# Router products on rows without their norm factor: a change to a two-layer trunk on one Trainium2 core

## The chip, the cores and the metric

The kernel runs on one core of one Trainium2 chip. The metric is the device time of one execution in microseconds (us). The engines are called as in the profile: PE is TensorE, DVE is VectorE, ACT is ScalarE, POOL is GpSimd, SP is SyncE. SP issues nearly all loads; ACT and POOL issue some transfers of their own.

## The reference

The model is a diffusion trunk of two layers over 512 latent and 256 context tokens of width 1024. Each layer mixes the tokens in four ways (attention, neighbourhood attention, a state-space scan, retention), projects the mix with `w_out`, adds it to the stream, and then sends every token to 2 of 32 experts. What the change touches is between the projection and the experts:

```python
xl = xl + gt1 * (jnp.concatenate([a_l, n_l, s_l, r_l], axis=-1) @ w_out[layer])
...
fl = rmsnorm(xl, g_ffn[layer]) * (1.0 + sc2) + sh2
...
def moe_ffn(h, w_group, b_group, w_expert, b_expert, w1, w3, w2):
    g_logits = jnp.matmul(h, w_group, preferred_element_type=F32) + b_group
    g_prob = jax.nn.softmax(g_logits, axis=-1)
    g_idx = jnp.argmax(g_logits, axis=-1)
    e_logits = (jnp.matmul(h, w_expert, preferred_element_type=F32) + b_expert).reshape(T, MOE_GROUPS, MOE_EXPERTS_PER_GROUP)
    e_logits = jnp.take_along_axis(e_logits, g_idx[:, None, None], axis=1)[:, 0]
    top_p, top_i = lax.top_k(jax.nn.softmax(e_logits, axis=-1), MOE_TOP_K)
...
        return (jax.nn.silu(xb @ w1[e]) * (xb @ w3[e])) @ w2[e]
```

`rmsnorm` divides a row by the root of its mean square, so `fl` is, row by row, `x * r * A2 + sh2` with one factor r per row and two vectors A2 and sh2 per layer and stream (latent or context). The router's 36 logits (4 groups, 4 x 8 experts) are `fl @ w_r + b_r`. All of it is in float32.

## The kernel before, in words

The stream lies in SBUF as row tiles of 128 tokens: six in layer 0 (four latent, two context), four in layer 1, where the context is no longer needed. A row tile is `xr`, 128 x 1024.

After the mixers, `w_out` (L1206 to L1245) is called for all row tiles with half 0 (columns 0 to 511 of the output), then for all with half 1. A call makes 24 products `wo_ps` of 128x512 (L202 to L204: each float32 operand is split into a high and a low part, and three products of the parts are added), multiplies by the gate `gt1` into the one buffer `wot` (L1223) and adds to `xr` (L1224). Half 1 goes on with the norm and the router. ACT squares the whole row into the new tile `h` and sums (L1229); DVE scales and adds epsilon (`rs_a`, L224), POOL raises to -1/2 (`rs_b`, L226); DVE makes h = x * r * A2 (L1231) and adds sh2 (L1232), 128x1024 each; ACT issues the write of the row tile `h` to the DRAM tensor `hd` (L1233), from which layer 0's experts gather their rows. In layer 1 the tile is also split into `hx`. PE transposes `h` in eight blocks (`h_t`, L1240), ACT copies them to `h2T` (L1242), eight products with the router weights `w_r` give `r_ps` (L1244), and DVE adds `b_r` into the logits `lgt` (L1245). The tile `h` has two buffers, taken in turn. A third writer of the same buffer waits until the readers of the first, the row write among them, are done.

The rows gt1, A2 and sh2 of each stream are loaded by SP from the DRAM tensor `md`, spread over all partitions (`mrow`, issued at the first call). Behind them on SP stand the expert weights: 1 MB tiles `ew` (L1406), six per expert. Some are loaded ahead into buffers that come free while `w_out` runs. Seven of them start when half 0 is done.

When all logits are there, `route` (L1266) runs on DVE: three times the first maximum of 4 or 8 values (`argmax`, L1247 to L1264, six operations: maximum, equal to it, two operations that turn the mask into an index or a large number, minimum, one-hot), softmax factors, counts and slots. A check for overflow reads a value to the engines' registers and branches (L1808, L1810), and the experts begin.

The order of the instructions on each engine isn't written by hand: a scheduler takes the program and arranges it, so the router work of a row tile is placed among the output products of the next.

## Time and profile before

| | |
|---|---|
| median of 3 runs | 2256.13 us (2254.74 to 2261.66) |
| profiled execution | 2260.11 us, span 2258.3 us |
| mean granted TensorE clock | 0.938 |
| busy: PE, DVE, ACT, POOL | 1955.8, 933.0, 499.6, 370.0 us |
| moved by the DMA engines | 578.55 MB, mean 256 GB/s |
| last output product of `w_out`, layer 0 and 1 | starts at 607.37 and 1720.13 us |
| first product of an expert in layer 0 | starts at 649.00 us |

A timeline row gives the start in us from the span's start, the duration, engine, line, operation, and in brackets the engine's idle time before it and what ended that. A windows row gives the busy time of each engine in a stretch. Granted clock is TensorE's, as a share of its full speed. A queue row (q1 SP's, q10 ACT's) gives the packets in a stretch, the MB, and their share of the time of the 16 DMA engines.

### The profile page before, as it was taken

The page shows a single profiled execution, that of the slowest core. Times are in us where ns is not written, and L with a number is a line of the kernel's source. Part 1 is how long each engine was busy: PE and PEld are TensorE (multiplying, and loading weights), DVE is VectorE, ACT ScalarE, POOL GpSimd, SP SyncE. Part 2 cuts the span into 40 slices and gives each one's busy share as a digit, 9 for nine tenths or more (in the row PEclk, how much of TensorE's full clock was granted, in tenths as well). Part 3 has the DMA queues.
Part 4 walks back from the last instruction along what each step waited for, and adds up shares of the span by engine and source line. Part 5 has one row for each costly group of instructions (what it writes and reads, how often), then busy time and mean ns, then how long its engine had stood idle before and what let it go on. Part 6 is the DMA issues. An engine that isn't in the chain of part 4 may idle for free. (4 is left out here: it accounts for less than half of the span.)

```text
span 2258.3 us, 32874 instructions
## 1 busy us (share of the span) xinstructions
PE 1955.8 (87%) x12609; PEld 1161.1 (51%) x12609; DVE 933.0 (41%) x2175; ACT 499.6 (22%) x1095; POOL 370.0 (16%) x396
## 2 busy tenths in 40 slices
PE   5897988899869879989887887988896898998996
PEld 2787865457733323333332687855475454444443
DVE  3758156463425411111111529056544353453444
ACT  3342232251202200000001521332432111111111
POOL 2532252120100000000001322253302000000000
PEclk9898999999979999999998988989997899999998
DMA  7351355562568999999998441355617599999996
GB/s 271 107 150 44 83 175 195 194 202 71 191 248 305 376 391 375 385 375 362 373 373 342 154 105 49 83 166 192 202 59 269 216 395 419 419 420 418 419 420 255
DMA packets 160477, 578.55 MB, mean 256 GB/s; under 512 B 30032, under 2 KB 71504, under 8 KB 111152
## 3 DMA queue, kind: packets, MB, share of 16 engines
q1 hardware_dynamic: 123344, 530.69, 61.8%
q10 hardware_dynamic: 31296, 31.36, 4.5%
q0 software_dynamic: 5664, 14.23, 2.2%
q8 instruction: 104, 1.70, 0.3%
q14 instruction: 69, 0.57, 0.1%
HBM read 536.33 MB, written 43.42 MB: 257 GB/s over the span
## 5 line engine op out<-in xcount | busy, mean ns | idle before, releaser
L1671 PE MATMUL e_pa<-ew,hT 128*64 128x512 f32 x1664 | 424.4, 605 | 39.0 <-DMA ew<-in_moe_w 32.5
L1671 PEld LDWEIGHTS e_pa<-ew,hT 128*64 128x64 f32 x1664 | 126.2, 139 | 299.0 <-issue 245.1
L1695 PE MATMUL e_py<-ew,aT 128*64 128x512 f32 x832 | 207.1, 632 | 10.6 <-DVE aT L1687 7.8
L226 POOL TENSOR_TENSOR rs_b<-rs_a,mhalf 128x1 f32<-128x1 f32 (+1 forms) x58 | 38.2, 658 | 834.5 <-DVE rs_a L224 829.5
L202 PE MATMUL nat_ps<-w_hi,hTh 128*128 128x272 f32 (+3 forms) x480 | 149.4, 311 | 9.0 <-ACT nat L190 5.5
L1676 ACT ACTIVATE sA<-e_pa 64x512 f32<-64x512 f32 x52 | 30.8, 592 | 564.0 <-PE e_pa L1671 549.9
L1677 DVE TENSOR_TENSOR sA<-sA,e_pa 64x512 f32<-64x512 f32 x52 | 35.9, 690 | 277.2 <-ACT sA L1676 276.7
L204 PE MATMUL nat_ps<-w_hi,hTl 128*128 128x272 f32 (+3 forms) x480 | 147.1, 306 | 0.0
L203 PE MATMUL nat_ps<-w_lo,hTh 128*128 128x272 f32 (+3 forms) x480 | 146.8, 306 | 0.0
L197 POOL TENSOR_TENSOR w_lo<-w_raw,w_hi 128x1024 fp32r<-128x1024 f32 (+2 forms) x36 | 89.9, 2509 | 234.2 <-ACT w_hi L196 109.7
L1695 PEld LDWEIGHTS e_py<-ew,aT 128*64 128x64 f32 x832 | 59.0, 143 | 113.9 <-issue 95.2
L1557 POOL DMA_INDIRECT hg<-hd,stok x32 | 31.3, 980 | 446.2 <-PE hg_t L1569 411.9
L202 PEld LDWEIGHTS nat_ps<-w_hi,hTh 128*128 128x128 f32 x480 | 98.9, 206 | 10.7 <-ACT nat L190 6.4
L296 PE MATMUL mod_ps<-wmod,cT 128*32 128x256 f32 x768 | 80.1, 444 | 27.2 <-DMA wmod<-in_w_mod 27.2
L192 DVE COPY hT<-hg_t 128x256 f32<-128x256 f32 (+2 forms) x45 | 24.0, 534 | 192.0 <-PE e_pa L1671 160.6
L203 PEld LDWEIGHTS nat_ps<-w_lo,hTh 128*128 128x128 f32 x480 | 98.7, 206 | 0.4 <-issue 0.4
L204 PEld LDWEIGHTS nat_ps<-w_hi,hTl 128*128 128x128 f32 x480 | 98.4, 205 | 0.2 <-issue 0.2
L203 PE MATMUL tr_ps<-hTl,w_hi 128*128 128x256 f32 (+1 forms) x256 | 88.1, 344 | 11.0 <-POOL hTl L486 10.6
L202 PE MATMUL tr_ps<-hTh,w_hi 128*128 128x256 f32 (+1 forms) x256 | 88.1, 344 | 5.4 <-DVE gT L583 3.3
L204 PE MATMUL tr_ps<-hTh,w_lo 128*128 128x256 f32 (+1 forms) x256 | 85.5, 334 | 0.0
L1017 PE MATMUL pT_ps<-const,sm_p 128*128 128x128 f32 x352 | 57.6, 292 | 18.4 <-DVE sm_p L1007 12.1
L1642 DVE TENSOR_TENSOR xr<-xr,po_ps 128x512 f32<-128x512 f32 x104 | 67.1, 684 | 7.7 <-PE po_ps L1640 7.1
(471 smaller groups left out, 3530.6 us busy)
## 6 DMA issues: line engine op xcount, KB each, us to landing
ew<-in_moe_w SPq DMA_DIRECT2D x384, 1024.0 KB
wmod<-in_w_mod SPq DMA_DIRECT2D x96, 512.0 KB
yd<-zero SPq DMA_DIRECT2D x20, 512.0 KB
w_raw<-in_w_in SPq DMA_DIRECT2D x16, 544.0 KB
w_raw<-in_w_in SPq DMA_DIRECT2D x16, 512.0 KB
w_raw<-in_w_out SPq DMA_DIRECT2D x32, 256.0 KB
yd<-yA ACTq DMA_DIRECT2D x64, 128.0 KB
hd<-h ACTq DMA_DIRECT2D x10, 512.0 KB
```

The lines of the kernel that those rows point to most:

```text
L197: (eng or self.nc.vector).tensor_tensor(out=lo, in0=src, in1=_f(hi), op=ALU.subtract)
L202: mm(out, lhsT=lh, rhs=rh, start=start, stop=False)
L203: mm(out, lhsT=lh, rhs=rl, start=False, stop=False)
L204: mm(out, lhsT=ll, rhs=rh, start=False, stop=stop)
L226: nc.gpsimd.tensor_tensor(out=r, in0=t, in1=self.mhalf[:, :n], op=ALU.pow)
L296: nc.tensor.matmul(ps[32 * j:32 * j + 32, 256 * q:256 * q + 256], lhsT=self.cT[:, k], rhs=w[:, j], start=(k == 0), stop=(k == KD - 1))
L1017: nc.tensor.transpose(pt[:, b], p[:, (a + b) * P:(a + b + 1) * P], self.ident)
L1557: self.nc.gpsimd.indirect_dma_start(out=hg, out_offset=None, in_=self.hd[0:n], in_offset=bass.IndirectOffsetOnAxis(ap=idx, axis=0), bounds ...
L1642: nc.vector.tensor_tensor(out=x, in0=x, in1=ps, op=ALU.add)
L1671: mm(pa[64 * j:64 * j + 64], lhsT=hT[k][:, 0:64], rhs=(w1, w3)[j][k], start=(k == 0), stop=(k == KD - 1))
L1677: nc.vector.tensor_tensor(out=sA, in0=sA, in1=pa[64:128], op=ALU.mult)
L1695: mm(py[64 * j:64 * j + 64, 0:512], lhsT=aT[:, k * 64:(k + 1) * 64], rhs=w2[k][:, h * 512:(h + 1) * 512], start=(k == 0), stop=(k == 3))
```

## The change

1. The transposes and router products take g = x * A2, without r and sh2. The logits are then r_ps * r + rb, where rb = sh2 @ w_r + b_r is one row of 36 per stream, on all partitions. g is made in two column halves. `h` is finished in the same tile, g * r + sh2, behind that.
2. The mean square is taken by column halves: ACT squares 128x512 after each half's addition, into the `wot` buffer; `ms2` keeps the first half's sum, DVE adds (`n_a`) and POOL raises (`n_b`).
3. rb is made in `router_bias`, at the first call: ACT issues a read of sh2 from `md` by columns, 128 x 8 single elements per stream (`sh2c`); DVE multiplies `w_r` by it (`rb_t`, 128x288) and sums over the eight blocks (`rb_v`, 128x36); a PE product with a matrix of ones sums over the partitions (`rb_ps`); DVE adds `b_r`. This is done twice in layer 0, once in layer 1.
4. `argmax` has five operations: the mask is multiplied by a constant row that counts down from 8, and the maximum taken. The indices, which nobody reads, aren't returned.

```diff
--- before.py
+++ after.py
@@ -75,6 +75,7 @@
     items["ident"] = np.eye(P)
     items["triu"] = (pos[:, None] < pos[None, :])
     items["iota"] = np.tile(pos[None, :], (P, 1))
+    items["down"] = np.tile(8 - np.arange(8)[None, :], (P, 1))
     items["tok"] = (np.arange(NT)[None, :] * P + pos[:, None]) - EMPTY
     e = np.arange(32)
     items["kadd"] = np.tile((np.where(e < NFIX, 1e6 * (NFIX - e), 0) - e)[None, :], (P, 1))
@@ -1210,7 +1211,11 @@
         TT = nc.vector.tensor_tensor
         c = slice(half * 512, half * 512 + 512)
         if i + half == 0:
-            self.mr = [[self.mrow(l, v, s, "%s%d" % (nm, s), wo) for v, nm in ((2, "gt1"), (4, "A2"), (3, "sh2"))] for s in range(2 if self.need_ctx else 1)]
+            ns = 2 if self.need_ctx else 1
+            self.mr = [[self.mrow(l, v, s, "%s%d" % (nm, s), wo) for v, nm in ((2, "gt1"), (4, "A2"), (3, "sh2"))] for s in range(ns)]
+            self.router_bias(wo, ns)
+            self.ms2 = wo.tile([P, NT], F32, name="ms2", bufs=1)
         gt1, A2, sh2 = self.mr[i >= LAT]
         tk = slice(i * P, (i + 1) * P)
         xt = self.xr[i]
@@ -1222,27 +1227,53 @@
         t = wo.tile([P, 512], F32, tag="wot", name="wot", bufs=1)
         TT(out=t, in0=ps, in1=gt1[:, c], op=ALU.mult)
         TT(out=xt[:, c], in0=xt[:, c], in1=t, op=ALU.add)
+        ss = wo.tile([P, 1], F32, tag="ss2", name="ss2")
+        nc.scalar.activation(out=t, in_=xt[:, c], func=AF.Square, accum_out=ss)
         if not half:
+            nc.vector.tensor_scalar(out=self.ms2[:, i:i + 1], in0=ss, scalar1=1.0 / D, scalar2=EPS, op0=ALU.mult, op1=ALU.add)
             return
-        h = wo.tile([P, D], F32, tag="h2", name="h2")
-        ss = wo.tile([P, 1], F32, tag="ss2", name="ss2")
-        nc.scalar.activation(out=h, in_=xt, func=AF.Square, accum_out=ss)
-        r = self.rsqrt(wo, ss, 1, 1.0 / D, "n2")
-        nc.vector.scalar_tensor_tensor(out=h, in0=xt, scalar=r, in1=A2, op0=ALU.mult, op1=ALU.mult)
-        TT(out=h, in0=h, in1=sh2, op=ALU.add)
-        nc.scalar.dma_start(out=self.hd[tk], in_=h)
-        if CAPS[l] == 64:
-            self.split(self.hx[i][0], self.hx[i][1], h, nc.gpsimd)
+        ra = wo.tile([P, 1], F32, tag="n2a", name="n2_a")
+        nc.vector.tensor_scalar(out=ra, in0=ss, scalar1=1.0 / D, scalar2=self.ms2[:, i:i + 1], op0=ALU.mult, op1=ALU.add)
+        r = wo.tile([P, 1], F32, tag="n2b", name="n2_b")
+        nc.gpsimd.tensor_tensor(out=r, in0=ra, in1=self.mhalf[:, :1], op=ALU.pow)
+        g = wo.tile([P, D], F32, tag="h2", name="h2")
+        for b in range(2):
+            d = slice(b * 512, b * 512 + 512)
+            TT(out=g[:, d], in0=xt[:, d], in1=A2[:, d], op=ALU.mult)
         ps = self.pM.tile([P, 512], F32, tag="lg", name="r_ps")
         for a in range(2):
             pt = self.pT.tile([P, 4, P], F32, tag="T", name="h2_t")
             for b in range(4):
-                nc.tensor.transpose(pt[:, b], h[:, (4 * a + b) * P:(4 * a + b + 1) * P], self.ident)
+                nc.tensor.transpose(pt[:, b], g[:, (4 * a + b) * P:(4 * a + b + 1) * P], self.ident)
             hT = wo.tile([P, 4, P], F32, tag="h2T", name="h2T")
             nc.scalar.copy(out=hT, in_=pt)
             for b in range(4):
                 nc.tensor.matmul(ps[:, :36], lhsT=hT[:, b], rhs=self.wr[:, 4 * a + b], start=(a + b == 0), stop=(a * 4 + b == KD - 1))
-        TT(out=self.lg[:, i], in0=ps[:, :36], in1=self.br, op=ALU.add)
+        nc.vector.scalar_tensor_tensor(out=self.lg[:, i], in0=ps[:, :36], scalar=r, in1=self.rb[i >= LAT], op0=ALU.mult, op1=ALU.add)
+        nc.vector.scalar_tensor_tensor(out=g, in0=g, scalar=r, in1=sh2, op0=ALU.mult, op1=ALU.add)
+        nc.scalar.dma_start(out=self.hd[tk], in_=g)
+        if CAPS[l] == 64:
+            self.split(self.hx[i][0], self.hx[i][1], g, nc.gpsimd)
+    def router_bias(self, wo, ns):
+        nc, l = self.nc, self.l
+        sc = wo.tile([P, ns, KD], F32, name="sh2c", bufs=1)
+        self.rb = []
+        ones = wo.tile([P, P], F32, name="ones32", bufs=1)
+        nc.gpsimd.memset(ones, 1.0)
+        for s in range(ns):
+            nc.scalar.dma_start(out=sc[:, s], in_=self.md[l][s, 3 * D:4 * D].rearrange("(k p) -> p k", p=P), allow_slow_non_contiguous=True)
+            t = wo.tile([P, 512], F32, tag="wot", name="rb_t", bufs=1)[:, :KD * 36].rearrange("p (k e) -> p k e", e=36)
+            nc.vector.tensor_tensor(out=t, in0=self.wr, in1=_bc(sc[:, s], [P, KD, 36], (2,)), op=ALU.mult)
+            v = wo.tile([P, 36], F32, tag="rbv", name="rb_v", bufs=1)
+            nc.vector.tensor_reduce(out=v, in_=t.rearrange("p k e -> p e k"), axis=AX.X, op=ALU.add)
+            pb = self.pM.tile([P, 512], F32, tag="lg", name="rb_ps")
+            nc.tensor.matmul(pb[:, :36], lhsT=ones, rhs=v, start=True, stop=True)
+            b = wo.tile([P, 36], F32, name="rb%d" % s, bufs=1)
+            nc.vector.tensor_tensor(out=b, in0=pb[:, :36], in1=self.br, op=ALU.add)
+            self.rb.append(b)
 
     def argmax(self, pool, v, n, m, tag):
 
@@ -1253,15 +1284,14 @@
         nc.vector.tensor_reduce(out=mxv, in_=v, axis=AX.X, op=ALU.max)
         c = pool.tile(sh, F32, name=tag + "c")
         TT(out=c, in0=v, in1=_bc(mxv, sh, (2,)), op=ALU.is_equal)
-        io = _bc(self.c("iota")[:, :m], sh, (1,))
-        f2 = lambda a: a.rearrange("p a b -> p (a b)")
-        nc.vector.tensor_scalar(out=f2(c), in0=f2(c), scalar1=-64.0, scalar2=64.0, op0=ALU.mult, op1=ALU.add)
-        TT(out=c, in0=c, in1=io, op=ALU.add)
+        io = _bc(self.c("down")[:, :m], sh, (1,))
+        TT(out=c, in0=c, in1=io, op=ALU.mult)
         ix = pool.tile([P, n], F32, name=tag + "ix")
-        nc.vector.tensor_reduce(out=ix, in_=c, axis=AX.X, op=ALU.min)
+        nc.vector.tensor_reduce(out=ix, in_=c, axis=AX.X, op=ALU.max)
         oh = pool.tile(sh, F32, name=tag + "oh")
         TT(out=oh, in0=io, in1=_bc(ix, sh, (2,)), op=ALU.is_equal)
-        return mxv, ix, oh
+        return mxv, oh
 
     def route(self, rp):
         nc = self.nc
@@ -1269,7 +1299,7 @@
         TT = nc.vector.tensor_tensor
         n = self.nt
         lg = self.lg[:, :n]
-        gm, gi, goh = self.argmax(rp, lg[:, :, 0:4], n, 4, "rg")
+        gm, goh = self.argmax(rp, lg[:, :, 0:4], n, 4, "rg")
         t4 = rp.tile([P, n, 4], F32, name="rt4")
         TT(out=t4, in0=lg[:, :, 0:4], in1=_bc(gm, [P, n, 4], (2,)), op=ALU.subtract)
         nc.scalar.activation(out=t4, in_=t4, func=AF.Exp)
@@ -1280,10 +1310,10 @@
         TT(out=sel, in0=lg[:, :, 4:36].rearrange("p i (g e) -> p i g e", g=4), in1=_bc(goh, [P, n, 4, 8], (3,)), op=ALU.mult)
         el = rp.tile([P, n, 8], F32, name="rel")
         nc.vector.tensor_reduce(out=el, in_=sel.rearrange("p i g e -> p i e g"), axis=AX.X, op=ALU.add)
-        m1, i1, oh1 = self.argmax(rp, el, n, 8, "r1")
+        m1, oh1 = self.argmax(rp, el, n, 8, "r1")
         f2 = lambda a: a.rearrange("p a b -> p (a b)")
         nc.vector.scalar_tensor_tensor(out=f2(el), in0=f2(oh1), scalar=-1e30, in1=f2(el), op0=ALU.mult, op1=ALU.add)
-        m2, i2, oh2 = self.argmax(rp, el, n, 8, "r2")
+        m2, oh2 = self.argmax(rp, el, n, 8, "r2")
         e2 = rp.tile([P, n], F32, name="re2")
         TT(out=e2, in0=m2, in1=m1, op=ALU.subtract)
         nc.scalar.activation(out=e2, in_=e2, func=AF.Exp)
```

The order on the engines, at three places. First PE in layer 0 at the start of `w_out`; wo_ps are output products, mixN and mixS parts of the mix. Before:

```order
L203 MATMUL wo_ps<-wol_4527,mixN 128x512
L204 MATMUL wo_ps<-woh_4525,mixN 128x512
L202 MATMUL wo_ps<-woh_4525,mixS 128x512
L203 MATMUL wo_ps<-wol_4527,mixS 128x512
L204 MATMUL wo_ps<-woh_4525,mixS 128x512
```

After:

```order
L204 MATMUL wo_ps<-wol_4527,mixN 128x512
L205 MATMUL wo_ps<-woh_4525,mixN 128x512
L1273 MATMUL rb_ps<-rb_v,ones_5244 128x36
L203 MATMUL wo_ps<-woh_4525,mixS 128x512
L204 MATMUL wo_ps<-wol_4527,mixS 128x512
L205 MATMUL wo_ps<-woh_4525,mixS 128x512
L203 MATMUL wo_ps<-woh_4525,mixS 128x512
L1273 MATMUL rb_ps<-rb_v,ones_5244 128x36
L204 MATMUL wo_ps<-wol_4527,mixS 128x512
```

Two products with ones now stand among the first output products, behind the twelfth and behind four more. In layer 1 one stands behind the twelfth.

Second, DVE in layer 0 from the second half of tile 0 to the logits of tile 1. The numbers at h and xr tell the row tiles apart: xr_4516, 4517, 4518 are tiles 0, 1, 2; h_5489, h_5552, h_5615 (before: h_5443, h_5505) are theirs. Before:

```order
L1223 TENSOR_TENSOR wot<-wo_ps,mrow_gt_5231 128x512
L1224 TENSOR_TENSOR xr_4516<-xr_4516,wot 128x512
L224 TENSOR_SCALAR rs_a<-ss_5444 128x1
L1231 SCALAR_TENSOR_TENSOR h_5443<-xr_4516,rs_b,mrow_A_5233 128x1024
L1232 TENSOR_TENSOR h_5443<-h_5443,mrow_sh_5235 128x1024
L1223 TENSOR_TENSOR wot<-wo_ps,mrow_gt_5231 128x512
L1224 TENSOR_TENSOR xr_4517<-xr_4517,wot 128x512
L1245 TENSOR_TENSOR lgt_4597<-r_ps,b_r 128x36
L224 TENSOR_SCALAR rs_a<-ss_5506 128x1
L1231 SCALAR_TENSOR_TENSOR h_5505<-xr_4517,rs_b,mrow_A_5233 128x1024
```

After:

```order
L1228 TENSOR_TENSOR wot<-wo_ps,mrow_gt_5231 128x512
L1229 TENSOR_TENSOR xr_4516<-xr_4516,wot 128x512
L1243 TENSOR_TENSOR h_5489<-xr_4516,mrow_A_5233 128x512
L1236 TENSOR_SCALAR n_a<-ss_5483,ms_5264 128x1
L1254 SCALAR_TENSOR_TENSOR h_5489<-h_5489,n_b,mrow_sh_5235 128x1024
L1253 SCALAR_TENSOR_TENSOR lgt_4597<-r_ps,n_b,rb_5253 128x36
L1228 TENSOR_TENSOR wot<-wo_ps,mrow_gt_5231 128x512
L1243 TENSOR_TENSOR h_5615<-xr_4518,mrow_A_5233 128x512
L1229 TENSOR_TENSOR xr_4517<-xr_4517,wot 128x512
L1243 TENSOR_TENSOR h_5552<-xr_4517,mrow_A_5233 128x512
L1236 TENSOR_SCALAR n_a<-ss_5546,ms_5264 128x1
L1254 SCALAR_TENSOR_TENSOR h_5552<-h_5552,n_b,mrow_sh_5235 128x1024
```

The one multiply with r and A2 is now two without r. The first of tile 2 (h_5615) stands between wot and xr of tile 1. The third h has the buffer of the first. The finishing operation (L1254) stands ahead of the logits (L1253). Layer 1 has the same order.

Third, PE in layer 0 behind the last output product; h_5691 is tile 4's tile, h_5753 and (after) h_5804 tile 5's. Before:

```order
L1240 MATMUL h_t<-const,h_5691 128x128 x8
L203 MATMUL wo_ps<-wol_4528,mixR 128x512
L204 MATMUL wo_ps<-woh_4526,mixR 128x512
L1244 MATMUL r_ps<-w_r,h2T 128x36 x8
L1240 MATMUL h_t<-const,h_5753 128x128 x8
L1244 MATMUL r_ps<-w_r,h2T 128x36 x8
```

After:

```order
L203 MATMUL wo_ps<-woh_4526,mixR 128x512
L204 MATMUL wo_ps<-wol_4528,mixR 128x512
L205 MATMUL wo_ps<-woh_4526,mixR 128x512
L1248 MATMUL h_t<-const,h_5804 128x128 x4
L1252 MATMUL r_ps<-w_r,h2T 128x36 x4
L1248 MATMUL h_t<-const,h_5804 128x128 x4
L1252 MATMUL r_ps<-w_r,h2T 128x36 x4
```

The products r_ps of tile 4 no longer stand behind the last output product, and tile 5's transposes and products come in two parts. In layer 1 the work of tile 2, which stood there in the same way, has moved ahead too.

## Rows read from the trace of the kernel before

**Rows 1.** Windows: stretch, length; busy PE, PEld, DVE, ACT, POOL; granted clock; DMA share; GB/s.

```profile
650.00:1230.00 580.00, 523.02 (x3214) 189.54 (x3210) 119.17 (x244) 61.94 (x133) 30.61 (x30) 0.97 0.95 367
1753.50:1765.00 11.50, 11.10 (x42) 6.95 (x44) 3.38 (x11) 3.07 (x4) 0.00 (x0) 0.77 0.00 0
1850.00:2233.00 383.00, 354.57 (x2379) 169.52 (x2378) 166.20 (x298) 44.70 (x79) 0.00 (x0) 1.00 1.01 417
```

**Rows 2.** Timeline of DVE, layer 0's end of w_out: start, us, instruction, [idle before, releaser].

```profile
607.80 0.69 DVE L1223 TENSOR_TENSOR wot<-wo_ps,mrow_gt 128x512 f32<-128x512 f32 x1 [2.03 <-PE wo_ps L204]
...
611.34 1.28 DVE L1231 SCALAR_TENSOR_TENSOR h<-xr,rs_b,mrow_A 128x1024 f32<-128x1024 f32 x1 [0.75 <-POOL rs_b L226]
...
619.52 0.20 DVE L1245 TENSOR_TENSOR lgt<-r_ps,b_r 128x36 f32<-128x36 f32 x1 [5.63 <-PE r_ps L1244]
...
620.18 0.18 DVE L1258 TENSOR_SCALAR rgc<-rgc 128x24 f32<-128x24 f32 x1
```

**Rows 3.** Timeline of PE, the same stretch.

```profile
607.37 0.40 PE L204 MATMUL wo_ps<-woh,mixR 128*128 128x512 f32 x1
607.61 1.96 PE L1244 MATMUL r_ps<-w_r,h2T 128*128 128x36 f32 x16
614.03 1.94 PE L1240 MATMUL h_t<-const,h 128*128 128x128 f32 x8 [4.46 <-DVE h L1232]
615.85 3.63 PE L1244 MATMUL r_ps<-w_r,h2T 128*128 128x36 f32 x16
```

**Rows 4.** Timeline of all engines, end of layer 1's w_out.

```profile
1720.13 0.39 PE L204 MATMUL wo_ps<-woh,mixR 128*128 128x512 f32 x1
...
1735.31 0.19 DVE L1245 TENSOR_TENSOR lgt<-r_ps,b_r 128x36 f32<-128x36 f32 x1 [5.65 <-PE r_ps L1244]
```

**Rows 5.** Timeline and windows (columns as in rows 1) where w_out begins, both layers.

```profile
528.00 0.27 ACT L196 CAST mixA<-a_o 128x128 fp32r<-128x128 f32 x1 [2.06 <-PE a_o L1119]
...
528.64 0.50 PE L202 MATMUL wo_ps<-woh,mixA 128*128 128x512 f32 x1 [0.68 <-DVE mixA L197]
...
1669.77 0.50 PE L202 MATMUL wo_ps<-woh,mixA 128*128 128x512 f32 x1 [0.68 <-DVE mixA L197]
...
531.55:534.50 2.95, 2.95 (x14) 2.40 (x13) 0.00 (x0) 0.00 (x0) 0.00 (x0) 1.00 0.97 408
534.50:536.00 1.50, 1.50 (x9) 1.19 (x8) 1.38 (x2) 0.00 (x0) 0.00 (x0) 1.00 0.16 60
1668.60:1671.30 2.70, 2.02 (x15) 1.50 (x12) 0.29 (x1) 0.27 (x1) 0.00 (x0) 1.00 0.91 376
1671.30:1674.00 2.70, 2.70 (x13) 2.20 (x12) 0.00 (x0) 0.00 (x0) 0.00 (x0) 1.00 0.00 0
```

**Rows 6.** Loads of short pieces: DMA queue 1584 to 1585 us; timeline of bglu.

```profile
q1 hardware_dynamic: 930, 0.13, 88.3%
...
1309.15 0.46 SPq L850 DMA_DIRECT2D bglu<-in_s_b_glu  x1
...
1312.71 0.17 DVE L851 TENSOR_SCALAR bglu<-bglu 128x2 f32<-128x2 f32 x1 [3.94 <-DMA bglu<-in_s_b_glu]
```

**Rows 7.** Windows at a lower clock; timeline of PE at the first experts.

```profile
611.60:612.60 1.00, 0.00 (x0) 0.00 (x0) 1.00 (x1) 0.00 (x0) 0.00 (x0) 0.61 0.50 130
649.00:652.00 3.00, 3.00 (x8) 1.09 (x10) 0.00 (x0) 0.00 (x0) 0.00 (x0) 0.50 0.60 186
...
649.00 5.51 PE L1671 MATMUL e_pa<-ew,hT 128*64 128x512 f32 x16 [6.49 <-PEq L1810]
...
656.30 3.65 PE L1671 MATMUL e_pa<-ew,hT 128*64 128x512 f32 x16
```

**Rows 8.** Tile 0's row write and its queue at 580:581; tile 1's at 581.8:585.2.

```profile
574.06 0.34 ACTq L1233 DMA_DIRECT2D hd<-h  x1
...
q10 hardware_dynamic: 66, 0.21, 51.5%
...
q10 hardware_dynamic: 144, 0.52, 38.2%
```


## Prediction

> **What bounds the kernel now.** I read the stretches of the trace first, then the timelines around the part that changes. In layer 0's experts TensorE is busy 523 of 580 us; in layer 1's the DMA engines stand still at first, since all buffers are full, and from 1850 us to the end they are at 1.01 of their share [rows 1]. In both layers the experts can only begin once the router has decided, and the router begins when the last logit row is written. Whatever moves that instant therefore moves the end, one for one: in layer 0 through TensorE, in layer 1 through expert weights that come later by as much, because each waits for a buffer that an expert frees.
>
> So two things count: when TensorE ends the last output product of `w_out`, and how long the last logit comes behind it. During `w_out` TensorE runs products without a gap, one each 0.23 us; a wait of TensorE there is lost.
>
> **The end of w_out.** In layer 0 the last product ends at 607.77 and the last logits at 619.72 [rows 2, 3], 11.95 us later. Between them stand 1.96 us of router products of tile 4, the two 128x512 operations, square sum and power, two 128x1024 operations (the first 1.28 us), the transposes at 614.03 after 4.46 us without work, and the products, which take 3.63 us where tile 4's took 1.96: the clock had dropped. In layer 1 it is 1720.52 to 1735.50, 14.98 us, as tile 2's transposes and products lie behind the last product as well [rows 4].
>
> After the change the transposes need only `x*A2`. Its first half is made ahead for each tile, so of the last tile there are wot 0.69, xr 0.72 and one half product 0.72 with their gaps: ready 2.2 us after the last product. The first half's transposes (0.5, as all eight took 1.94 at half clock), ACT copy and products run in those 2.2 us, the products ending about at 2.4. Then second transposes 0.5, copy 0.7, products 1.0 and the logit operation with gaps 0.4: 5.0 us, all at the full clock since the gaps are short. The last product itself comes later by what moved ahead of it: in layer 0 1.96 of tile 4, plus 0.6 for five tiles whose router work is now cut into four pieces, less the 0.42 us for which TensorE waited at the first transposes: 2.1 us. Gain 11.95 - 5.0 - 2.1 = **4.8 us**. In layer 1 what moves ahead is 1.0 + 1.96, plus 0.4, less 0.5: 2.9, gain 14.98 - 5.0 - 2.9 = **7.1 us**. The power of the mean square is off this path: it must be there at the logit operation only.
>
> **The maxima.** Three times per layer one DVE operation on the path goes; it takes 0.18 us [rows 2]: 6 x 0.18 = **1.1 us**.
>
> **The router bias.** This is new work that TensorE waits for. ACT issues the read of sh2 by columns after its last cast of mixA (528.00, so about 528.3, 0.3 us ahead of TensorE's first output product at 528.64 [rows 5]; in layer 1 by the same step about 1669.4, ahead of 1669.77). TensorE reaches the new product after 12 output products, 12 x 0.23 later plus a little: about 531.5 and 1672.6. Price of the read: 1,024 pieces of 4 bytes. The nearest rows: the router weights, 1,024 short pieces too, moved 930 of them in 1 us; a read of 256 single elements was issued at 1309.15 and used at 1312.71, 3.56 us [rows 6]. In quiet I take 3.3 us to landing, just under those 3.56, the lower bound. It is not quiet in layer 0: the engines are at 0.97 until 534.50, full of SP's rows and expert weights, and at 0.16 behind that [rows 5]. I take it that the column read gets through when the load ends: landing 536.4. In layer 1 the load (0.91) ends by 1671.30 and then is 0.00: landing about 1673.6. DVE then needs a multiply of 288 and a sum over 288 values per partition, which I put at 0.5 us each, between the 0.18 of a small operation and the 0.69 of one with 512 [rows 2]. Stall in layer 0: 537.4 - 531.5 = **6.0 us**, in layer 1 1674.6 - 1672.6 = **2.0 us**; lower bounds by a quiet read 1.1 and 0.3. The products with ones, two and one, with the second chain behind the first: **0.5 and 0.3 us**.
>
> The Trainium skill, "DMA: Bandwidth & Descriptors", section "Rules for kernel authors", speaks against this read: a strided last dimension becomes one descriptor per element, and the advice is to rearrange it. No run so far has a read of 1,024 single elements; by its fixed cost of some 2.0 us (section "Anatomy of one DMA") an estimate would be 2.0 plus 1.1 us, close to what I took for quiet.
>
> **The clock.** TensorE idle from 609.57 had the granted clock 0.61 in 611.60 to 612.60, about 2 us later; back at work after a long wait it had 0.50 (1.2 GHz) for 3 us, and the first 16 expert products took 5.51 us where the next took 3.65 [rows 7]. A stall much over 2 us thus costs 1.9 us more: layer 0's bias stall, **1.9 us**; layer 1's, at the edge, none.
>
> **The row write of tile 0.** There are two h2 buffers. The first-half multiply of tile 2 needs the buffer of tile 0, free when tile 0's row write has landed, and DVE has it queued ahead of `xr` of tile 1. So behind that wait stand xr 0.69, the second half multiply of tile 1, and TensorE's transposes of it. Call T0 the end of tile 0's second half (568.0; 1697.9). Before, the write was issued at 574.06 while seven expert tiles of 1 MB were loading (until T0 + 12.3); 66 of its 144 packets moved only at 580 to 581, with half of the engines' share, so it took 7 us and its landing; tile 1's write, in quiet, moved all 144 from 581.80 to 585.20 [rows 8]. After the change the write comes behind wot, xr, a half product, square, power and one 128x1024 operation: T0 + 5.1. As the loads still run, I put its landing at T0 + 13.4. Then 0.69 + 0.72 + 0.72 + 0.1: transposes possible at T0 + 15.65. TensorE reaches them at about T0 + 12.0 (tile 1's products 5.6, tile 0's router work 2.9, then half of tile 2's): stall **3.7 us** in layer 0, **3.45** in layer 1, and **1.9 us** of clock behind each. Lower bound nothing, if the write lands by T0 + 9.5. Later tiles have this multiply behind their `xr`, and their writes land in quiet: nothing.
>
> **Nothing for** the twelve smaller ACT squares, the split at layer 1 and the memset: these engines are far from full there, and the next wot comes 5 us later. If that cover went, each square would cost its 0.7 us once.
>
> **Sum.** Gains 4.8 + 7.1 + 1.1 = 13.0. Losses: bias 6.0 + 0.5 + 1.9 + 2.0 + 0.3 = 10.7; row write 3.7 + 3.45 + 3.8 = 10.95; together 21.65. Net +8.6 us. The profiled execution took 2260.11 us (its span 2258.3), so 2268.7 for it; the median of the runs is 2256.13, 4 us below, and against that I forecast **2265 us**. With all lower bounds (bias 1.1 + 0.3 + 0.8, no row wait) the sum is -10.8, with read and gain at their worst about +18.
>
> **Rivals.**
> A. Both waits bite as above: +8.6, 2265. For it: the full engines in both places, and the 7 us of that row write. Chance 0.50.
> B. The column read shares the engines with SP's traffic: the row write had half the share while weights still ran [rows 8]. At half share its 1.1 us of pieces take 2.2, landing 533.4; the stall is 2.9 and the clock loss a third. Net about +4, 2260, within 0.3% (6.8 us, about what a measurement of this kernel can tell from no change). Chance 0.15. The Trainium skill, same page, section "Queues, rings and completion order", has such a rule: each engine takes the queues in turn, packet by packet. The row write's packets beside the weights agree in part only: they came 3 us late.
> C. The row write lands early enough, or DVE's queue is late anyway, so that only the bias waits: 8.6 - 10.95 = -2.4, 2254, the same. Against it: the 7 us of the write before. Chance 0.13.
> D. **The other side, faster**: ACT's transfers get through beside SP's loads as if alone. Then both row waits vanish and the bias stalls are 1.1 and 0.3 us: -10.8, 2245. It decides at the landing of tile 0's write: under some 4.5 us after its issue. For it: the 3.4 us of a quiet write; against: the one row write whose packets I followed under load. Chance 0.10.
> E. Pieces of 4 bytes cost three times those of 144: both bias stalls grow by 2 to 4 us and layer 1's costs clock too: +15 to +18, 2273. Chance 0.12.
>
> **Numbers.** 2250 to 2273 takes in A, B, C and most of E and leaves D out, with some of E. Faster by over 0.3%: D and the edge of C, 0.13. Same: B, C and the lower edge of A, 0.33. Slower: A and E, 0.54.
>
> **What would show it.** In the changed profile: the first new product of layer 0 should stand behind an idle stretch of about 6 us, waiting for DVE's rb_v and that for a DMA of sh2c; layer 1's behind 2 us. DVE's first-half multiply of tile 2 should wait some 3 to 4 us for hd, with TensorE idle after it, and granted clock 0.50 behind each. The last logits should come 5 us behind the last output product. I am wrong if sh2c lands under 4 us after its issue in layer 0, if that multiply doesn't wait, or if TensorE has other work queued in the gap.

## The result and the profile after

The changed kernel takes 2271.86 us in the median of 14 runs (2264.82 to 2279.87); the kernel before, in 14 runs, 2261.68 (2254.30 to 2267.40). The ratio is 1.0054, with a 95% interval of 1.0041 to 1.0067: it is slower, by 9 to 15 us. The profiled execution took 2279.87 us (span 2278.1, mean clock 0.931), the slowest of the 14, so I read stretches in it and not its end.

Page of the changed kernel: busy time by engine, DMA packets, ACT's queue.

```profile
PE 1962.9 (86%) x12615; PEld 1161.6 (51%) x12615; DVE 943.4 (41%) x2198; ACT 504.2 (22%) x1115; POOL 366.3 (16%) x398
...
DMA packets 163597, 578.56 MB, mean 254 GB/s; under 512 B 33152, under 2 KB 74624, under 8 KB 114272
...
q10 hardware_dynamic: 34416, 31.37, 4.5%
```

The busy time hardly shows it: PE has 7 us more, DVE 10. Over 3,000 packets more come from the column reads, 1,024 single elements for each of three streams.

Timeline of DVE in the changed kernel, layer 0's `w_out` (start, us, instruction, [idle before, releaser]):

```profile
536.10 0.46 DVE L1269 TENSOR_TENSOR rb_t<-w_r,sh2c 128x288 f32<-128x288 f32 x1 [7.73 <-DMA sh2c<-md]
536.59 0.64 DVE L1271 TENSOR_REDUCE rb_v<-rb_t 128x36 f32<-128x288 f32 x1
...
584.90 0.69 DVE L1228 TENSOR_TENSOR wot<-wo_ps,mrow_gt 128x512 f32<-128x512 f32 x1 [2.82 <-PE wo_ps L205]
589.78 0.69 DVE L1243 TENSOR_TENSOR h<-xr,mrow_A 128x512 f32<-128x512 f32 x1 [4.19 <-DMA hd<-h]
590.39 0.68 DVE L1229 TENSOR_TENSOR xr<-xr,wot 128x512 f32<-128x512 f32 x1
591.11 0.69 DVE L1243 TENSOR_TENSOR h<-xr,mrow_A 128x512 f32<-128x512 f32 x1
```

Both waits that the prediction named are there. `rb_t` begins at 536.10, after 7.73 us, with the column read (forecast 536.4). The half of tile 2's multiply that stands ahead of tile 1's `xr` waits for tile 0's row write until 589.78, 13.1 us behind T0 (576.65), forecast 13.4.

Queues of SP (q1) and ACT (q10) in the changed kernel, 533 to 534 and 534 to 535 (packets, MB, share of the 16 engines' time):

```profile
q1 hardware_dynamic: 53, 0.43, 102.4%
q10 hardware_dynamic: 52, 0.00, 2.9%
...
q1 hardware_dynamic: 40, 0.23, 54.8%
q10 hardware_dynamic: 843, 0.00, 47.4%
```

Beside the loads the two queues moved nearly one packet for one, 53 and 52, though ACT's packets are single elements of 4 bytes: 52 of the 2,048 elements of both reads in one us. As the loads ran out in the next, 843 went.

Timeline of PE: the first new product, tile 1's second transposes, and the end of layer 0's `w_out`:

```profile
537.38 0.61 PE L1273 MATMUL rb_ps<-rb_v,ones 128*128 128x36 f32 x2 [4.35 <-DVE rb_v L1271]
...
591.95 1.09 PE L1248 MATMUL h_t<-const,h 128*128 128x128 f32 x4 [3.61 <-DVE h L1243]
...
625.50 0.39 PE L205 MATMUL wo_ps<-woh,mixR 128*128 128x512 f32 x1
625.74 0.60 PE L1248 MATMUL h_t<-const,h 128*128 128x128 f32 x4
627.06 1.08 PE L1252 MATMUL r_ps<-w_r,h2T 128*128 128x36 f32 x8 [0.73 <-ACT h2T L1250]
628.22 0.63 PE L1248 MATMUL h_t<-const,h 128*128 128x128 f32 x4
629.58 1.08 PE L1252 MATMUL r_ps<-w_r,h2T 128*128 128x36 f32 x8 [0.73 <-ACT h2T L1250]
```

PE stands 4.35 us for the bias and 3.61 for the transposes. At the end the chain runs as it was costed. The last output product ends at 625.89, and the DVE timeline has the last logits at 630.95, 5.06 us later (11.95 before, by [rows 2, 3]), and rM, which opens the counting of slots, 5.35 us behind them (5.86 before):

```profile
630.70 0.25 DVE L1253 SCALAR_TENSOR_TENSOR lgt<-r_ps,n_b,rb 128x36 f32<-128x36 f32 x1 [0.25 <-PE r_ps L1252]
...
636.30 0.36 DVE L1332 TENSOR_TENSOR rM<-rOH 128x192 bf16<-128x192 f32 x1
```

Granted clock in the changed kernel (columns as in [rows 1]):

```profile
528.40:532.00 3.60, 3.58 (x9) 2.82 (x10) 0.00 (x0) 0.00 (x0) 0.00 (x0) 0.54 0.82 307
532.00:537.00 5.00, 1.02 (x4) 0.50 (x3) 0.86 (x2) 0.00 (x0) 0.00 (x0) 0.84 0.76 222
537.00:539.00 2.00, 1.62 (x5) 1.46 (x6) 1.46 (x4) 0.00 (x0) 0.00 (x0) 0.50 0.00 0
...
588.00:592.00 4.00, 0.39 (x3) 0.09 (x2) 2.06 (x4) 0.72 (x2) 0.00 (x0) 0.77 0.27 111
592.00:593.00 1.00, 1.00 (x5) 1.00 (x6) 0.14 (x1) 0.00 (x0) 0.55 (x1) 0.50 0.00 0
593.00:594.00 1.00, 1.00 (x4) 0.81 (x3) 0.86 (x1) 0.59 (x1) 0.00 (x0) 0.50 0.00 0
594.00:596.00 2.00, 2.00 (x10) 1.81 (x9) 0.42 (x1) 0.00 (x0) 0.00 (x0) 0.50 0.36 145
596.00:598.00 2.00, 2.00 (x7) 1.61 (x7) 0.26 (x1) 0.00 (x0) 0.00 (x0) 0.50 0.29 117
598.00:600.00 2.00, 2.00 (x6) 1.60 (x5) 0.00 (x0) 0.00 (x0) 0.00 (x0) 0.50 0.00 0
600.00:620.00 20.00, 20.00 (x117) 16.55 (x116) 10.89 (x18) 5.12 (x11) 1.08 (x2) 0.99 0.13 53
```

Behind the row wait the clock is 0.50 from 592 to 600. There products come 0.43 us apart instead of 0.23. The clock was 0.54 at the start of `w_out` too, before any new wait; the experiments come back to that.

Timeline of the changed kernel in layer 1, all engines:

```profile
1685.68 0.46 DVE L1269 TENSOR_TENSOR rb_t<-w_r,sh2c 128x288 f32<-128x288 f32 x1 [2.60 <-DMA sh2c<-md]
...
1725.91 0.69 DVE L1243 TENSOR_TENSOR h<-xr,mrow_A 128x512 f32<-128x512 f32 x1 [4.80 <-DMA hd<-h]
...
1728.08 1.09 PE L1248 MATMUL h_t<-const,h 128*128 128x128 f32 x4 [3.96 <-DVE h L1243]
...
1744.62 2.36 POOL L198 TENSOR_TENSOR hx<-h,hx 128x1024 fp32r<-128x1024 f32 x1
...
1745.38 0.69 DVE L1228 TENSOR_TENSOR wot<-wo_ps,mrow_gt 128x512 f32<-128x512 f32 x1 [2.13 <-PE wo_ps L205]
...
1745.99 1.03 DVE L1399 TENSOR_TENSOR rrd<-rprow,rrf 128x8 f32<-128x8 f32 x1
...
1751.10 0.26 DVE L1253 SCALAR_TENSOR_TENSOR lgt<-r_ps,n_b,rb 128x36 f32<-128x36 f32 x1 [0.39 <-PE r_ps L1252]
...
1752.23 2.36 POOL L198 TENSOR_TENSOR hx<-h,hx 128x1024 fp32r<-128x1024 f32 x1 [2.84 <-ACT hx L197]
1752.42 2.32 DVE L1310 TENSOR_TENSOR rsel<-lgt,rgoh 128x128 f32<-128x128 f32 x1
```

The bias and the row write of tile 0 wait here too (2.60 and 4.80 us on DVE). New is the last pair. While POOL makes the low part of the last tile's split, 2.36 us, DVE's `rsel` takes 2.32 us. It lies on the path between the last logits and the experts. Timeline of the kernel before:

```profile
1736.78 0.29 DVE L1280 TENSOR_TENSOR rsel<-lgt,rgoh 128x128 f32<-128x128 f32 x1
```

By stretches of each profile, before and after (us; in layer 1 the experts' first product is `g_ps`, which picks the expert's rows):

| | layer 0 | layer 1 |
|---|---|---|
| to the first wot | 5.91, 14.75 | 5.90, 7.08 |
| tile 1's wot to tile 2's, half 1 | 9.32, 15.98 | 8.67, 16.45 |
| last product to last logits | 11.95, 5.06 | 14.98, 6.02 |
| last logits to rM | 5.86, 5.35 | 5.31, 6.82 |
| first product of `w_out` to first expert's | 120.36, 130.53 | 83.79, 87.33 |

The last row is the sum: +10.2 in layer 0, +3.5 in layer 1, 13.7 us, beside 12.2 (9 to 15) by the ratio.

### The profile page after: what moved, and what is told of

It is laid out like the page before. It is cut to its first block, busy times and chain, and to the rows that moved or that the text cites. A ratio compares the mean times of both kernels' runs of the same rounds, so it can differ in the third digit from the quotient of the medians.

```text
span 2278.1 us, 32952 instructions
## 1 busy us (share of the span) xinstructions
PE 1962.9 (86%) x12615; PEld 1161.6 (51%) x12615; DVE 943.4 (41%) x2198; ACT 504.2 (22%) x1115; POOL 366.3 (16%) x398
## 5 line engine op out<-in xcount | busy, mean ns | idle before, releaser
L227 POOL TENSOR_TENSOR rs_b<-rs_a,mhalf 128x1 f32<-128x1 f32 (+1 forms) x48 | 32.9, 685 | 659.0 <-DVE rs_a L225 654.1
L203 PEld LDWEIGHTS nat_ps<-w_hi,hTh 128*128 128x128 f32 x480 | 97.2, 202 | 14.1 <-ACT nat L191 7.9
L204 PE MATMUL tr_ps<-hTl,w_hi 128*128 128x256 f32 (+1 forms) x256 | 88.0, 344 | 12.2 <-POOL hTl L487 11.8
```

Of the source, the lines that this page charges most:

```text
L203: mm(out, lhsT=lh, rhs=rh, start=start, stop=False)
L204: mm(out, lhsT=lh, rhs=rl, start=False, stop=False)
```

## Experiments

Theory: the late column read (9 us in layer 0, 1 in layer 1) and the wait for tile 0's row write (some 8 us in each layer) are two separate losses, and the tail's gain is real. Rivals: the low clock ahead of the first wait is the loss there, not the wait; the row write holds up whoever needs its buffer next, so that nothing is gained by a later multiply; layer 1's experts swallow what `w_out` gains or loses. All ratios are to the kernel before, with their 95% intervals.

**The column read, early.** The read stands on SP right behind the router weights:

```diff
 (w_out_load)
+        for s in range(2 if self.need_ctx else 1):
+            nc.sync.dma_start(out=self.sc[:, s], in_=self.md[l][s, 3 * D:4 * D].rearrange("(k p) -> p k", p=P), allow_slow_non_contiguous=True)
 (router_bias)
-            nc.scalar.dma_start(out=sc[:, s], in_=self.md[l][s, 3 * D:4 * D].rearrange("(k p) -> p k", p=P), allow_slow_non_contiguous=True)
```

> The change with one edit: the columns of sh2 are read by SP right behind the router weights, long before w_out, instead of by ACT when w_out begins. Theory: the late column read alone makes TensorE wait in w_out's first tile. Then in layer 0 the first wot comes 6.0 to 6.7 us after the first output product (14.75 us in the changed kernel, 5.9 before), in layer 1 6.0 to 6.5 (7.08; 5.9 before); everything else stays, the whole is about 9 us shorter than the changed kernel, so 1 to 4 us over the kernel before. Rival: the slow clock that the changed kernel's profile shows from 528 us on, ahead of the wait, is a cost of its own; then the first wot still comes 9 us or later after the first product and the gain is 4 to 5 us.

Measured 1.0014 (0.9998 to 1.0030): some 9 us less than the changed kernel. PE no longer waits for the bias. Yet the first wot comes 8.64 us after the first product in layer 0 (6.21 in layer 1). Windows of this run:

```profile
526.00:528.00 2.00, 1.32 (x6) 0.80 (x4) 1.07 (x3) 0.27 (x1) 0.00 (x0) 0.50 1.04 313
528.00:530.00 2.00, 2.00 (x8) 1.61 (x7) 1.00 (x3) 0.00 (x0) 0.00 (x0) 0.50 1.00 307
530.00:532.00 2.00, 2.00 (x7) 1.71 (x6) 0.20 (x1) 0.00 (x0) 0.00 (x0) 0.50 1.05 442
532.00:534.00 2.00, 2.00 (x9) 1.61 (x9) 0.00 (x0) 0.00 (x0) 0.00 (x0) 0.90 0.44 180
```

There was no wait here, and the clock was still 0.50 from 526 to 532. So both readings had a part: the wait was most of the loss, and a low clock at this place cost some 2 us (8.64 against 6.59 in the run with both edits below, where the clock stayed at 1.00). The changed kernel's wait had hidden them, since PE only came to the same wait later.

**One multiply for x*A2.** The early half goes everywhere:

```diff
-        for b in range(2):
-            d = slice(b * 512, b * 512 + 512)
-            TT(out=g[:, d], in0=xt[:, d], in1=A2[:, d], op=ALU.mult)
+        TT(out=g, in0=xt, in1=A2, op=ALU.mult)
```

> The change with one edit: x*A2 is one 128x1024 multiply again, not two halves, so nothing of a later tile can be made ahead. Theory: DVE's wait for tile 0's row write comes from the half made ahead. Then that wait goes in both layers, the step from tile 1's wot to tile 2's is 8.3 to 8.6 us (15.98 and 16.45 in the changed kernel), TensorE keeps its clock there, and the logits come 5.8 to 6.2 us behind the last output product (5.06): about 13.5 us shorter than the changed kernel, 1 to 4 us under the kernel before. Rival: the row write holds the buffer for whoever comes next, so the wait moves to the multiply of tile 2 itself and TensorE waits 2 us or more one tile later; gain under 7 us. Second rival: layer 1's experts, which wait for their weights, swallow layer 1's part; gain 7 to 8 us.

Measured 1.0009 (0.9996 to 1.0021), some 10 us less than the changed kernel where 13.5 was expected. DVE waits for no row write in either layer. Timeline of DVE, tile 1's wot, its multiply, tile 2's wot:

```profile
581.40 0.69 DVE L1228 TENSOR_TENSOR wot<-wo_ps,mrow_gt 128x512 f32<-128x512 f32 x1 [1.90 <-PE wo_ps L205]
...
582.85 1.23 DVE L1241 TENSOR_TENSOR h<-xr,mrow_A 128x1024 f32<-128x1024 f32 x1
...
589.99 0.69 DVE L1228 TENSOR_TENSOR wot<-wo_ps,mrow_gt 128x512 f32<-128x512 f32 x1 [1.91 <-PE wo_ps L205]
```

The step is 8.59 us, as expected, where it was 15.98. The tail was misjudged: the logits come 8.60 and 9.39 us behind the last product, not 6. PE stands 2.86 us at the transposes in layer 0 and 3.65 in layer 1, and works at a clock of 0.50 behind that: the sixteen router products take 3.63 us in either layer, where two groups of eight took 1.08 each in the changed kernel's layer 0. The waits are gone (7.6 and 8.1 us, worked out below), the tail is 3.5 and 3.4 us longer; the whole stretches are 127.24 and 83.37 us, 7.3 less in sum than the changed kernel's. That is the second rival's number but not its reason: 4.0 of it are layer 1's, so its experts swallowed little. The wait did not move to another tile.

**Halves for the last tile alone.**

```diff
-        for b in range(2):
-            d = slice(b * 512, b * 512 + 512)
+        nb = 2 if i == self.nt - 1 else 1
+        for b in range(nb):
+            d = slice(b * D // nb, (b + 1) * D // nb)
```

> The change with one edit: only the last tile's x*A2 is made in two halves, the other tiles' in one. Theory: the wait for the row write goes as in the run with one multiply everywhere, and the logits still come 5.0 to 5.3 us behind the last output product: 14 to 15 us shorter than the changed kernel. Rival: the half of the last tile waits for a row write too; then its tail is longer than 5.5 us.

Measured 1.0004 (0.9987 to 1.0020), about 11 us less than the changed kernel; 14 to 15 lies at the interval's edge. Layer 0's tail is 5.07 us, no row wait is left. Layer 1's tail is 7.16, outside the 5.0 to 5.3 that were expected, and not by the rival's row wait: `rrd` was held for 1.00 us there too, and the clock was 0.50 from the second transposes on, so that the last eight router products took 1.92 us instead of 1.08. Behind the logits it was `rgc` here that met the split. Timeline of layer 1 (PE, POOL, DVE):

```profile
1733.23 1.92 PE L1253 MATMUL r_ps<-w_r,h2T 128*128 128x36 f32 x8 [0.73 <-ACT h2T L1251]
...
1735.42 2.34 POOL L198 TENSOR_TENSOR hx<-h,hx 128x1024 fp32r<-128x1024 f32 x1 [3.17 <-ACT hx L197]
...
1735.69 2.10 DVE L1287 TENSOR_TENSOR rgc<-lgt,rgmx 128x16 f32<-128x16 f32 x1
```

All five profiles with halves for the last tile alone have these 1.92 us in layer 1, and their tails there are 6.7 to 7.2 us; in the four with halves everywhere the products took 1.08 to 1.21, and the tails are 5.9 to 6.0. Why the clock falls there in one form and not in the other is open.

**The last tile's split on DVE**, layer 1:

```diff
-            self.split(self.hx[i][0], self.hx[i][1], g, nc.gpsimd)
+            self.split(self.hx[i][0], self.hx[i][1], g, nc.vector if i == self.nt - 1 else nc.gpsimd)
```

> The change with one edit: in layer 1 the low part of the last tile's split is made by DVE instead of POOL. Theory: in the changed kernel rsel takes 2.32 us instead of 0.29 because POOL's 2.36 us split runs beside it and DVE must wait for it. Then rsel is back to 0.29, DVE has one more operation of 1.2 to 1.3 us, and from the last logits to rM it takes 6.0 to 6.3 us (6.82 in the changed kernel, 5.31 before): under 1 us in the whole, not to be seen in the time. Rival: rsel waits for something else, ACT's cast beside it for one; then it stays over 1 us.

Measured 1.0047 (1.0032 to 1.0062), the changed kernel's time. Timeline of DVE:

```profile
1748.99 0.29 DVE L1310 TENSOR_TENSOR rsel<-lgt,rgoh 128x128 f32<-128x128 f32 x1
...
1750.72 1.22 DVE L198 TENSOR_TENSOR hx<-h,hx 128x1024 fp32r<-128x1024 f32 x1
```

`rsel` is back to 0.29, and logits to rM take 5.82 us, a little under the 6.0 to 6.3 expected. It is POOL's split that held DVE, and whichever operation with two SBUF operands comes first is held until the split ends: `rsel` in one run, `rgc` in another, and for 1.03 us `rrd` (0.16 before); the wot beside the same split, with one operand in PSUM, ran its usual 0.69. The Trainium skill, "GPSIMD Engine Reference", section "1. Specifications", says that GpSimd's SBUF interfaces are shared with VectorE, with contention for DVE operations with two SBUF inputs; the rows agree, 2.32 against 0.29 us.

**Both edits**, the early read and the halves for the last tile, each as in its diff above:

> The change with both edits: the early column read, and halves for the last tile alone. Theory: the two waits are separate, their gains add. Without them layer 0's stretch from the first output product to the first expert product is 115.8 us (118.2 if the clock is low at its start as in the run with the early read; 120.36 before, 130.53 in the changed kernel), layer 1's 79 us (83.79 before): 7 to 9.5 us under the kernel before, a ratio of 0.996 to 0.997. Rival: layer 1's experts wait for weights in any case, so only layer 0's 2 to 4.5 us are seen, ratio 0.998 to 0.999.

Measured 0.9976 (0.9960 to 0.9991). Layer 0's stretch is 117.17 us and layer 1's 78.77, together 8 us under before. Against the changed kernel that is 13.4 us less in layer 0, where the edits alone gave 5.7 and 7.3, and 8.6 in layer 1, where they gave 3.5 (2.3 of it because the clock came back sooner behind the row wait, which the other edit takes away) and 7.4. So the gains add, and up to the first expert product layer 1's are not swallowed. The ratio says 5.4 us (2 to 9), between the theory's and the rival's, so it can't tell whether the experts give some of it back; and this profile is of the fastest of the 12 runs. The clock at the start was 1.00 in it. Layer 0's tail is 5.91 here, as the clock fell to 0.50 in it and the last router products took 1.92 us.

**Both edits, and the last two splits on DVE:**

```diff
-            self.split(self.hx[i][0], self.hx[i][1], g, nc.gpsimd)
+            self.split(self.hx[i][0], self.hx[i][1], g, nc.vector if i >= self.nt - 2 else nc.gpsimd)
```

> As the run with both edits, and in layer 1 the low parts of the last two tiles' splits are made by DVE instead of POOL. Theory: DVE's operations with two SBUF operands wait while POOL's split runs; without that rrd of the last tile is 0.16 us instead of 1.03, no operation of route lasts over 0.5 us but the split itself (1.22), and layer 1's stretch from the last output product to rM is 1 to 2 us shorter than in the run with both edits: ratio 0.9955 to 0.9965. Rival: what DVE saves it gives back by making the splits itself; then the stretch is as long as in the run with both edits.

Measured 0.9997 (0.9983 to 1.0011), so not better. `rrd` and `rsel` were no longer held, and from the last product to rM it is 12.86 us instead of 13.58, but from rM to the first expert 13.85 instead of 11.46. DVE's two splits, 1.22 us each, stand in the tail and in `route` instead. Layer 1's stretch is 80.47, worse than the rival had it.

**The five-operation maximum alone**, on the kernel before:

```diff
-        nc.vector.tensor_scalar(out=f2(c), in0=f2(c), scalar1=-64.0, scalar2=64.0, op0=ALU.mult, op1=ALU.add)
-        TT(out=c, in0=c, in1=io, op=ALU.add)
+        TT(out=c, in0=c, in1=io, op=ALU.mult)
...
-        nc.vector.tensor_reduce(out=ix, in_=c, axis=AX.X, op=ALU.min)
+        nc.vector.tensor_reduce(out=ix, in_=c, axis=AX.X, op=ALU.max)
```

> The kernel before with the five-operation first maximum alone. Theory: from the last logits to rM 0.5 to 0.6 us less per layer, 5.2 to 5.35 and 4.7 to 4.8 (5.86 and 5.31 before), nothing else changes, and the whole is not to be told from the kernel before. Rival: another operation is on the path there, and the interval stays within 0.2 us.

Measured 0.9987 (0.9970 to 1.0004). Logits to rM take 5.20 and 4.68 us, 0.66 and 0.63 less. Its profile also has a low clock at the start of layer 0's `w_out`, windows:

```profile
526.00:528.00 2.00, 0.94 (x7) 0.70 (x8) 0.62 (x2) 0.27 (x1) 0.00 (x0) 0.91 1.05 369
528.00:530.00 2.00, 2.00 (x5) 1.53 (x5) 0.00 (x0) 0.00 (x0) 0.00 (x0) 0.50 1.01 272
530.00:532.00 2.00, 2.00 (x8) 1.63 (x7) 0.00 (x0) 0.00 (x0) 0.00 (x0) 0.74 1.04 426
```

Its first wot comes after 7.34 us. Nothing of `w_out` is changed in this kernel, so a low clock there doesn't need the change.

**The kernel before once more**, no edit:

> The kernel before, unchanged, for a second profile of it. Theory: the low clock at the start of layer 0's w_out, in all five profiles of changed kernels and not in the one of the kernel before, comes by chance from the short products ahead of it, which are the same in all; then this profile or that of the five-operation maximum shows a granted clock of 0.50 for some us near 528 too, and the first wot comes 8 us or more after the first product. Rival: the change brings it; then both show 1.00 there and 5.9 us.

Measured 1.0004 (0.9989 to 1.0020). This profile shows 1.00 there and 5.90 us; so the change alone does not decide it. Of the 14 profiles of the study eight have the low clock there and six have not: seven of the ten with the change in `w_out`, one of the four without. That is too few to tell whether the change makes it more frequent.

**Five buffers in layer 1's second pool**, on the changed kernel:

```diff
-    NB = ((7, 4, 3), (7, 6, 0))
+    NB = ((7, 4, 3), (7, 5, 0))
```

> The change with one edit: in layer 1 the second pool of expert weight buffers has five tiles instead of six, so five loads stand ahead of the overflow branch. Theory: layer 1's first expert does not wait for the router but for these loads: the last of them get their buffers when POOL's split of the last tile ends (1754.59; issues from 1754.62), they drain by 1766.3, the code behind the branch comes only then, and the first expert product starts 4 us later. One load less drains 2.4 us earlier: from the first of the last loads' issue to the first expert product 13.2 to 13.7 us (15.85 in the changed kernel, 15.85 and 15.68 in two others). Rival: the branch takes its 5.8 to 8.9 us from the position's arrival whatever the loads do; then that stretch stays at 15.5 or more. Of the whole time neither says much: the load comes later instead.

Measured 1.0040 (1.0023 to 1.0056). The stretch asked for was 15.55 us, so by its number the theory fell. The loads show why it said little: in the changed kernel one of the six had already gone ahead of the logits, here none had, and five were issued from the logits on in both. The DMA engines worked until 1754 here and until 1766.4 in the changed kernel, and the first expert product came 4 us later in both, at 1757.92 and 1770.47. That agrees with the theory's path, but shows it no better than the stretch does.

**The split first, on DVE** (both parts, behind the last logits, with both edits):

```diff
+            if i == self.nt - 1:
+                nc.vector.tensor_copy(self.hx[i][0], g)
+                nc.vector.tensor_tensor(out=self.hx[i][1], in0=g, in1=_f(self.hx[i][0]), op=ALU.subtract)
+            else:
```

> As the run with both edits (early column read, halves for the last tile alone), and in layer 1 DVE makes both parts of the last tile's split right behind the last logits, ahead of route. Theory: the split's end, not the logits, releases the last weight loads in layer 1, and their drain sets the first expert: the split ends 1.5 to 2.2 us earlier behind the last output product (9.2 in the run with both edits), and so does the first expert product (25.04 there), though rM comes about 1 us or more later behind the logits than in the kernel before. Layer 1's stretch 76.5 to 77.5 us (78.77); the whole 1 to 2 us under the run with both edits, ratio 0.9965 to 0.998. Rival: route is the bound; then the first expert comes as late as there or later by what DVE does more, 78.8 to 80 us.

Measured 0.9953 (0.9935 to 0.9971), the best ratio of the study, though its interval meets that of the run with both edits. Layer 1's stretch is 78.56 us, 0.2 less than 78.77. The split ended 9.02 us behind the last output product, 9.16 in the run with both edits, so the theory's condition, a split that ends 1.5 us earlier, did not come about, and the run decides nothing between theory and rival. I claim for it only what both edits give.

**Two buffers in layer 1's second pool**, in the kernel with both edits and two splits on DVE, and in the one with the five-operation maximum alone:

```diff
-    NB = ((7, 4, 3), (7, 6, 0))
+    NB = ((7, 4, 3), (7, 2, 0))
```

> The run with both edits and DVE splits for the last two tiles, with only two tiles, not six, in layer 1's second pool of expert buffers. What is still open: route ends earlier there, but the first expert does not come earlier (8.87 us from the arrival of the largest position, mp_f, against 7.36 in the changed kernel). Theory: the code behind the branch gets through only when the loads ahead have drained; with two loads there is nothing left by then, and from mp_f to layer 1's first expert product it is 6.0 to 6.6 us, as in layer 0 (5.8 to 6.5). Rival: the branch itself takes that long; then 8.5 us or more. With fewer buffers the experts behind it may be slower; the whole time is not what is asked.

> The kernel before with the five-operation first maximum, and two tiles in layer 1's second pool. Theory: from mp_f to layer 1's first expert product 6.0 to 6.6 us instead of 8.62, so that the 0.6 us saved on DVE reach the first expert. Rival: 8.5 us or more.

Both take 1.009 of the time before (1.0057 to 1.0116, two runs each); that the experts have fewer buffers is the likely reason, not tested. The stretch from `mp_f` to the first expert is 6.26 us in the second (8.62 with six tiles). From the last logits it is 15.91 us, where the five-operation maximum with six tiles had 18.28 and the kernel before 18.06: with the loads gone the 0.6 us of the maxima, and 1.5 more, reach the expert. In the first it is 7.38 (8.87), between the two readings; its two loads ran until 1734.0 us and `mp_f` came at 1734.07. So the loads ahead of the branch do lengthen it; by which path (the code behind it, or a register) the runs don't tell.

## Why the prediction was right and wrong

It was right in sign and in that both waits bite, and the range held the median, though six of the 14 runs lie above its 2273. The size was off, and two steps failed: the clock behind the row write was priced too low, and the split at layer 1 was put at nothing. The forecast was +8.6 us on the profile, +8.9 from the median of three runs; the ratio says +12.2 (9 to 15). Against the later median of 2261.68 the 2265 was only 3.3 us up, so the base was part of the miss: three runs were too few for an absolute number. By its steps:

- **The tail.** Forecast 5.0 us behind the last product; measured 5.06 in layer 0. "All at the full clock since the gaps are short" held here, but not in every run: with both edits layer 0's tail met 0.50. The last product moved by 1.9 (forecast 2.1): gain 5.0 against 4.8. In layer 1 it is 6.0 instead of 5.0, since `rrd` met POOL: 6.5 against 7.1.
- **The maxima.** 1.1 us forecast, 1.3 measured alone.
- **The router bias.** 8.4 and 2.3 us forecast, 8.8 and 1.2 measured. DVE's moment was right to 0.3 us. PE's wait itself was 4.35, not 6.0, as PE came 1.7 us late under a low clock that I had not foreseen; that the sum still came out near 8.4 is luck in part. Layer 1's read was used 2.5 us behind the first output product (forecast 3.8), so rival E (dearer pieces) is out. In layer 0 it landed only when the load ended, not at 533.4 as rival B had it: B gave the read half of the engines' time, but the rows of the queues show half of the packets, and its packets are far smaller. Two small sums don't come out: a quiet read in layer 1 gives 1669.4 + 3.3 + 1.0 - 1672.6 = 1.1 us, not 0.3, and B's own terms land at 528.3 + 3.3 + 1.1 = 532.7. Neither enters the forecast. The 2.0 us of the estimate from the Trainium skill ("DMA: Bandwidth & Descriptors", section "Anatomy of one DMA") stands there for DMAs issued from POOL, and this read is ACT's. Layer 1's read was issued at 1682.50 and used at 1685.68, 3.2 us later.
- **The row write: the step that was mis-sized.** The waits were 3.6 and 4.0 us (3.7 and 3.45 forecast). "1.9 us of clock behind each" was wrong: the low clock lasted 8 us in layer 0, and the whole step cost 15.98 - 8.35 = 7.6 and 16.45 - 8.37 = 8.1 us (less the step of the tiles behind it; in layer 1 less the mean of the two other steps, 8.24 and 8.50) instead of 5.6 and 5.35. The 1.9 came from the experts' start [rows 7]; here output products 0.43 us apart instead of 0.23, for 8 us, are 3.7 us. In two other profiles layer 1's step was 14.1 and 14.2 with the same wait of PE, 4.3 and 4.2 us: there the clock was back at 1.00 about 3 us behind the wait. So the 1.9 us fit a clock that comes back so soon, as in two of the four profiles that have this wait in layer 1 and in none of the four in layer 0; which of the two comes, no run explains.
- **"Nothing for the split at layer 1": the step that failed outright.** I looked at how full POOL is, not at what it holds up. The finishing operation moved behind the transposes, so POOL's split moved out of a stretch where DVE waited for PE and into `route`: 2.0 us, and 0.9 more for `rrd`. The run with the split on DVE showed it for the 2.0; the `rrd` of the run with the last two splits on DVE, 0.15 us, for the 0.9.
- **"One for one" in layer 1.** Behind the logits stand the weight loads that `w_out`'s buffers release. With two buffers in that pool the branch is up to 2.4 us shorter; so a microsecond won on DVE there can be lost again, as the 0.6 us of the maxima alone were. For the larger shifts (both edits: 5 us) it held up to the first expert product; further no stretch was read.

Against the forecast, then: +4.75 us for the row write with its clock (15.7 for 10.95), +2.1 from the logits to rM, +0.4 for the tails, -0.7 for the bias, -1.5 in the rest of the stretches (rM to the first expert above all): 13.7 where 8.6 stood.

## What to carry to other kernels

Where a multiply is cut so that half of it can go ahead, look at whose buffer it needs and what stands behind it on its engine: made ahead for the last tile alone, the same halves gave layer 0's whole gain without the row wait, and all but some 1 us of layer 1's, which a lower clock took. A small strided read issued at the moment its consumer starts pays for everything that is loading then; put far ahead it cost no wait. Price a stall of TensorE together with the half-rate products behind it, and for work on POOL ask which two-operand DVE operations run beside it.

## What the runs showed of the hardware that I had not expected

- TensorE's granted clock fell to 0.50 at the start of layer 0's `w_out` in some profiles and stayed at 1.00 in others, with the same products ahead of it (short ones, with gaps of 0.5 to 0.7 us). Where nothing else waits, the first wot then comes after 7.3 to 8.6 us instead of 5.8 to 6.6.
- DVE operations as small as 128x16 (`rgc`, 0.17 us alone) took 2.10 us beside POOL's split.
- Beside each other two queues moved about as many packets, whatever their size: 53 of SP's loads and 52 of ACT's 4-byte elements from 533 to 534, 35 and 34 (the row write's) from 587 to 588.
- A row write of 512 KB issued at 581.45 beside expert loads held its buffer until 589.7; the same write in quiet moved in 3.4 us [rows 8].
